# A later start for the splits of the last operands, a written order for the first tiles, and earlier requests for the gate's weights, in a one-layer decoder block

## The chip, the cores and the metric

The kernel runs on one core of one Trainium2 chip. The core has a matrix engine (TensorE), a vector engine (VectorE), an activation engine (ScalarE), a general one (GpSimd) and a queueing engine (SyncE) that here issues all transfers. The metric is the device time of one execution in microseconds (us), lower is better. Three timed runs of the kernel before gave 1779.38, 1779.62 and 1783.3 us; the median is 1779.62 us.

## The reference

One layer of a hybrid decoder on x of 1024 tokens by 1024 channels in float32:

```
u = rmsnorm(h, mix_pre_norm);  z = u @ w_in
o_attn = dilated_attention_branch(z_attn)      # 3 head groups, (window, dilation) (128,1), (512,4), (2048,16)
o_rwkv = rwkv7_time_mix(z_rwkv, ...)           # delta-rule state update, 8 heads of 64
gate_attn, gate_rwkv = split(sigmoid(z_gate), 2)
merged = gate_attn * (o_attn @ w_attn_up) + gate_rwkv * (o_rwkv @ w_rwkv_up)
h = h + rmsnorm(merged @ w_out, mix_post_norm)
f = rmsnorm(h, ffn_pre_norm)
f = square(relu(f @ w_ff_in)) @ w_ff_out       # 1024 -> 4096 -> 1024
h = h + rmsnorm(f, ffn_post_norm)
e = (p @ w_ple) * sigmoid(h @ w_ple_gate)      # p: 1024 x 256
h = h + rmsnorm(e, ple_post_norm)
```

## The kernel before

**Products in split parts.** A float32 operand is kept as a pair: hi, a copy rounded to the type fp32r, and lo, the rest. A product is three passes, hi·hi, lo·hi and hi·lo (lines 292, 294 and 296). A pair of a weight is made by ScalarE, which copies (hi), and GpSimd or VectorE, which subtracts (lo); wload (line 313) does this for one tile of 128 x 1024 (512 KB). Part of the second product of the MLP is done by a fast scheme with seven products for eight: product(n) (line 1546) takes pairs that prep (line 1536) makes of sums, in the tags Ep, En, a for the left side and kk, MP, px for the right side, taken in turn by n mod 3. The last two of the 32 row tiles of w_ff_out aren't in that scheme: ff2_last (line 1625) multiplies them in three passes.

**Stages, in time.** Head, 0 to about 35 us: the eight tiles of x are loaded, normalised and transposed (lines 354 to 437). Then the projections, the RWKV recurrence and the attention, to about 785 us. Then merge (line 1272), the product with w_out, ff1 (line 1563) with the products of the MLP's second half beside it, to about 1634 us. Then the end: ff2_last for eight token tiles, finish(i) (line 1710: norm, the residual h from scratch, transposition), gate_mm(i) (line 1730: the gate's product, 8 k-tiles in two halves of 512 columns) and e_mm(i) (line 1749: the last product, norm and output).

**The head.** stats(i) (line 387) squares tile i on ScalarE with its sum, and takes the root there and the reciprocal on VectorE. u_tile(i) (line 393) scales the tile by both on VectorE, has TensorE transpose it in two groups of four blocks (tp), and takes uh (ScalarE) and ul (VectorE) from each. z_quarter(n, q) (line 406) multiplies 256 tokens by the n-th of the first two weight tiles. keep_warm puts in small matmuls.

**Who sets the order.** TensorE's order over the whole kernel is planned by the program: bodies of matmuls (sch.add) and chains of other work (sch.spawn) are generators, the classes Engine and Loads (lines 79 to 133) add up modelled times for the other engines, and the next body or chain is picked by these. The order in which instructions stand in the source is that in which the plan reaches them. The other four engines keep that source order in two stretches alone: between the end of the head (lines 1227 and 1228) and the start of attention() (line 991), and from ff2_last(0, 0) (line 1635) to the end of the program. Elsewhere a scheduler orders them by its own rule from the source position and the state of their inputs and buffers.

**Parking.** Fourteen operands of the last stages are split long before they are used, by park() (line 968): two tiles of w_ple, two halves of p transposed, two tiles of w_ff_out and eight of w_ple_gate. Each is loaded raw into tag MP, split into a pair in tag BK2, and the pair is stored in a scratch tensor in device memory: pk[1] (in the profile pke), pk[2] (pkl) and pk[0] (pkg). The chain starts when ("vk", 1) is done: turn(1) (line 1015) of attention sets this when the second group of values is transposed into vkb. The event ("B", n) is set by values() at line 1113, when the last product po of values group n is done; merge also waits for ("B", 5) (line 1310).

**What is read back at the end.** last_split(1, ..) (line 1498) asks for the second row tile of w_ff_out: hi in a tag lw, and lo, "lwl", in tag MP. It is called behind product(103) (n == 7·NP − 9, NP = 16), in the last ff1 body. Inside ff2_last(0, 0) the program calls hl_load(0) (the residual tile, line 1706), opens the second stretch of source order, and calls last_weights (line 1658), which makes the tiles wpg for the gate's weights (first half of the columns in the tags TM0 and TM1, second half in mtile) and starts a chain that asks for their sixteen parts of 512 KB, first half first, paced by the modelled bus. When a half has landed it sets ("wpg", c); gate_mm waits for these.

Of the kernel before, what the change touches and what calls it, by code (L numbers as in the profile page):

```python
# [18 lines left out]
D = 1024  # L19
# [225 lines left out]
def layer(ctx: ExitStack, tc: tile.TileContext, x, pT, wz, wup, w_out, wff1, w_ff2, w_ple, w_pleg,  # L245
# [58 lines left out]
    def wait(cond):  # L304
        while not cond():
            yield 0.1
# [47 lines left out]
    with tc.tile_pool(name="xin", bufs=1) as xp:  # L354
        xts = [xp.tile([128, D], F32, name=f"xt{i}") for i in range(8)]

        def load_x(*tiles):
            for i in tiles:
                SY.dma_start(xts[i], x[i * 128:(i + 1) * 128, :])

        g1 = xp.tile([1, D], F32, name="g1")
        SY.dma_start(g1, gains[0:1, :])
        load_x(0, 1)
        cs = const.tile([128, N_CS0], F32, name="cs")
        SY.dma_start(cs, cst[:, 0:N_CS0])
        ident = cs[:, C_ID:C_ID + 128]
        eps = cs[:, C_EPS:C_EPS + 1]
        one = xp.tile([128, 128], F32, name="one")
        V.memset(one, 1.0)
        warm = xp.tile([1, 128], F32, name="warm")  # L370
        S.activation(warm, one[0:1], AF.Sqrt)
        def keep_warm(n):
            keep = zbank()[:, 0:128]
            for i in range(n):
                mm(keep, one, one, 0.107)

        keep_warm(4)
        g0 = xp.tile([128, D], F32, name="g0")
        for b, c in enumerate((slice(0, 512), slice(512, 1024))):
            ps = psum.tile([128, 512], F32, name="gb", tag=f"s{b + 2}")  # L380
            mm(ps, one[0:1], g1[:, c], 0.86)
            V.tensor_copy(g0[:, c], ps)
        keep_warm(7)
        tp = [0]
        ub = {}

        def stats(i):
            ss = small.tile([128, 1], F32, name="ss")
            us = xp.tile([128, D], F32, name="us", bufs=4)
            S.activation(us, xts[i], AF.Square, accum_out=ss)  # L390
            ub[i] = us, rstd_of(ss, "rs")

        def u_tile(i):
            h, ts = i // 4, slice((i % 4) * 128, (i % 4) * 128 + 128)
            us, r = ub[i]
            V.scalar_tensor_tensor(us, xts[i], r, g0, op0=OP.mult, op1=OP.mult)
            for b in range(2):
                ps = psum.tile([128, 4, 128], F32, name="tp", tag=("m0", "m1", "s1", "s2")[tp[0] % 4])
                tp[0] += 1
                for k in range(4):  # L400
                    tr(ps[:, k, :], us[:, (4 * b + k) * 128:(4 * b + k + 1) * 128], 0.11)
                o = (slice(None), slice(4 * b, 4 * b + 4), ts)
                S.activation(uT[0][h][o], ps, AF.Copy)
                V.tensor_tensor(uT[1][h][o], ps, uT[0][h][o], OP.subtract)

        def z_quarter(n, q):
            h, ts = q // 2, slice((q % 2) * 256, (q % 2) * 256 + 256)
            if q % 2 == 0:
                zl[h].append(psum.tile([128, 512], F32, name="z", tag="s3") if h and n else zbank())
            hi, lo = wl[n]  # L410
            now(mm3(zl[h][n][:, ts], [(hi[:, k * 128:k * 128 + 128], lo[:, k * 128:k * 128 + 128],
                                       uT[0][h][:, k, ts], uT[1][h][:, k, ts]) for k in range(KT)]))

        stats(0)
        stats(1)
        wl = [wload(wz[0])]
        load_x(2)
        u_tile(0)
        u_tile(1)
        keep_warm(2)  # L420
        stats(2)
        wl.append(wload(wz[1]))
        load_x(3, 4, 5, 6, 7)
        pr = const.tile([128, N_PRM], F32, name="pr")
        SY.dma_start(pr, prm)
        omu = const.tile([128, 14], F32, name="omu")
        V.tensor_scalar(omu, pr[:, 0:14], -1.0, 1.0, op0=OP.mult, op1=OP.add)
        oka = const.tile([128, NU], F32, name="oka")
        V.tensor_scalar(oka, pr[:, P_KA:P_KA + NU], -1.0, 1.0, op0=OP.mult, op1=OP.add)
        for q in range(4):  # L430
            z_quarter(0, q)
            for i in (2 * q + 2, 2 * q + 3):
                if i < 7:
                    stats(i + 1)
                if i < 8:
                    u_tile(i)
            z_quarter(1, q)

    rt = ctx.enter_context(tc.tile_pool(name="rt", bufs=1, reuse_waits="tile"))
    TAGN = {"BT": 2048, "TM0": 4096, "TM1": 4096, "AR0": 2048, "AR1": 2048, "BK": 2048, "BK2": 2048, "UV": 2048,  # L440
# [526 lines left out]

    def park():

        yield from wait(lambda: ("vk", 1) in done)  # L970
        rows = lambda w, k: w[k * 128:(k + 1) * 128, :]
        half = lambda h: pT[:, halves[h]].rearrange("(k p) c -> p k c", p=128)
        for dst, src in ([(pk[1][:, k], rows(w_ple, k)) for k in range(2)]
                         + [(pk[1][:, 2 + h], half(h)) for h in range(2)]
                         + [(pk[2][:, k], rows(w_ff2, FF // 128 - 2 + k)) for k in range(2)]
                         + [(pk[0][:, k], rows(w_pleg, k)) for k in range(KT)]):
            raw = rtile([128, 1024], "pkr", "MP")
            land = SY.dma_start(raw if len(src.shape) == 2 else k2(raw), src)
            yield max(land - sch.t, 0.0)
            t = rtile([128, 2, 1024], "pk", "BK2", F32R)  # L980
            S.activation(t[:, 0], raw, AF.Copy)
            yield 1.0
            V.tensor_tensor(t[:, 1], raw, t[:, 0], OP.subtract)
            yield sch.until(V.end)
            yield max(SY.dma_start(dst, t.bitcast(F32)) - sch.t, 0.0)
            yield 3.0
        done.add("park")

    def attention():
# [573 lines left out]
    def ff1(j):  # L1563
        def body(hi, lo):
# [4 lines left out]
            for h in range(0 if j > 2 else 1, 2):  # L1569
                ps = zbank()  # L1570
                g = ff1_half(ps, hi, lo, h)
                for k in range(2):
                    for _ in range(12):
                        yield next(g)
                    if k:
                        for _ in g:
                            pass
                        ff1_evac(ps, j, h)
                    for n in [x for _ in range(1 if j > 2 else 2) for x in (next(muls, None),) if x is not None]:
                        yield from product(n)  # L1580
                        if n in E_LOADS:
                            e_weights(E_LOADS.index(n))
                        if n == 7 * NP - 10:
                            last_split(0, (0, 1), (0,))
                        if n == 7 * NP - 9:
                            last_split(1, (0,), (1,))
# [38 lines left out]
    def ff2_last(i, c):  # L1625
        def body():
# [3 lines left out]
                                 last[k][1][:, halves[c]]) for k in range(2)])  # L1630
            V.tensor_tensor(acc(i, c), acc(i, c), ps, OP.add)
            if i + c == 0:
                hl_load(0)
                sch.exact = True
                last["turn"] = tc.manual_schedule(engines=OTHERS)
                last["turn"].__enter__()
# [11 lines left out]
    def e_weights(n):  # L1648
# [6 lines left out]
        else:  # L1655
            P[f"p{n - 2}"] = [k2(t[:, 0]), k2(t[:, 1])]

    def last_weights():
        pg = pieces(GA, "wpg", F32R)
        P["wpg"] = [[Split(pg[4 * p:4 * p + 4]), mtile("hl"[p], 0, [128, KT, 512], "wpg", F32R)]  # L1660
                    for p in range(2)]
        P["g3"] = rtile([128, D], "g3", "v")
        SY.dma_start(P["g3"], gains[3:4, :].to_broadcast([128, D]))

        def chain():
            land = 0.0
            for c in range(2):
                for k in range(0, KT, 2):
                    for p in range(2):
                        w = P["wpg"][p][c]  # L1670
                        yield max(SY.bus - 2.0 - sch.t, 0.0)
                        land = SY.dma_start((w.p[k // 2] if c == 0 else w[:, k:k + 2, :]).bitcast(F32),
                                            pk[0][:, k:k + 2, p, halves[c]])
                yield max(land - sch.t, 0.0)
                done.add(("wpg", c))
            e_weights(3)
        sch.spawn(chain(), 2)

# [51 lines left out]
    def gate_mm(i):  # L1730
        def body():
# [2 lines left out]
            hi, lo, t0 = hT[i]  # L1734
            wpg = P["wpg"]
            for c in range(2):
                while ("wpg", c) not in done:
                    yield 0.0
                ps = zbank()
                yield from mm3(ps, [(hi[:, k, :], lo[:, k, :], wpg[0][c][:, k, slice(0, 512)],  # L1740
# [3 lines left out]
                warm = small.tile([128, 1], F32, name="ss")  # L1744
                S.activation(warm, P["sg"][i % 4][:, D - 1:D], AF.Sqrt)
            done.add(("G", i))
        sch.add(body, None, lambda: ("wpg", 0) in done and i in hT and sch.t >= hT[i][2])

    def e_mm(i):
        def body():  # L1750
# [3 lines left out]
            for n, c in enumerate(cols):  # L1754
# [7 lines left out]
                S.activation(junk, sg[:, c], AF.Square, accum_out=sc[:, n:n + 1])  # L1762
                if n == 0 or i < 7:
                    (V if n else G).tensor_tensor(eg[:, c], sg[:, c], P["g4"][:, c], OP.mult)
            for c in cols[1:] if i == 7 else ():
                V.tensor_tensor(eg[:, c], sg[:, c], P["g4"][:, c], OP.mult)
            for n in range(1, len(cols)):
                V.tensor_tensor(sc[:, n:n + 1], sc[:, n - 1:n], sc[:, n:n + 1], OP.add)
            r = rstd_of(sc[:, n:n + 1], "rs")
            for c in cols:  # L1770
                V.scalar_tensor_tensor(sg[:, c], eg[:, c], r,
                                       acc(i, c.start // 512)[:, c.start % 512:(c.stop - 1) % 512 + 1], op0=OP.mult, op1=OP.add)
# [132 lines left out]
```

## Time and profile before

| what | us |
|---|---|
| median of three runs | 1779.62 |
| lowest and highest run | 1779.38, 1783.3 |
| the profiled execution | 1784.63 |
| its span (first to last instruction) | 1782.8 |
| mean granted TensorE clock | 0.993 of full |

All rows of the profile are of the one profiled execution, so their times add up to its span. A row of the timeline has the start, the duration, the engine, the line, the operation with output and inputs, the shapes, and in brackets the idle time of its engine just before and what ended it. "xN" is a count of instructions in the row. PE is TensorE, PEld its loading of weights, DVE VectorE, ACT ScalarE, POOL GpSimd, SPq the queue of SyncE. Line 113 is the helper through which all instructions of VectorE, ScalarE and GpSimd pass, and line 132 that of the transfers, so groups are told apart by the names of their tiles. A row of the waits says which instruction of TensorE waited for which engine's work, how long in total, how many times, and the longest.

### The profile page before, as it was taken

Reading aid. Unit: us, or ns where it says so; the run is one execution under the profiler, and the core shown is the slowest. Engines: PE = TensorE matmul, PEld = TensorE weight load, DVE = VectorE, ACT = ScalarE, POOL = GpSimd, SP = SyncE. Lnnn points to the kernel's source line nnn. Section 1 sums busy time; section 2 is a strip of 40 time slices with the busy share of each in tenths; the row PEclk is TensorE's granted clock in tenths of the full one; section 3 lists DMA queues with packets and bytes.
Section 4 is the critical chain, followed back from the end, with each engine's and each line's share of the span. In section 5 each row is a group of like instructions: output and inputs, shape, how many; then the busy total and the mean of one; then the engine's idle time right before and its main releaser. Section 6 shows DMA issues by size and latency. Waiting matters only on the chain. (4 is left out here: it accounts for less than half of the span.)

```text
span 1782.8 us, 25896 instructions
## 1 busy us (share of the span) xinstructions
PE 1751.7 (98%) x10192; PEld 1431.0 (80%) x10192; DVE 1069.6 (60%) x1880; ACT 733.1 (41%) x1301; POOL 735.0 (41%) x485
## 2 busy tenths in 40 slices
PE   9999989999999999999999999999999999999998
PEld 8787877878877777777888888888888888888786
DVE  6289776757546343342744655565565677888643
ACT  5833333332345444452533533333333333333353
POOL 1354131221222323322230276666666797893211
PEclk9999999999999999999999999999999999999999
DMA  4621121212375543232632321111211121114611
GB/s 162 210 95 36 49 77 43 90 42 91 111 246 191 183 166 95 84 133 104 208 132 97 110 80 51 48 55 41 76 55 48 48 72 48 48 36 165 219 48 47
DMA packets 59322, 175.49 MB, mean 98 GB/s; under 512 B 6849, under 2 KB 7233, under 8 KB 56898
## 3 DMA queue, kind: packets, MB, share of 16 engines
q1 hardware_dynamic: 59202, 173.85, 29.0%
q8 instruction: 80, 1.31, 0.3%
q14 instruction: 40, 0.33, 0.1%
HBM read 125.20 MB, written 41.94 MB: 94 GB/s over the span
## 5 line engine op out<-in xcount | busy, mean ns | idle before, releaser
L113 DVE TENSOR_TENSOR tot<-tot,bk 128x512 f32<-128x512 f32 x468 | 308.1, 684 | 190.6 <-PE bk L296 189.8
L113 POOL TENSOR_TENSOR wl<-wr,wh 128x1024 fp32r<-128x1024 f32 (+1 forms) x87 | 211.5, 2431 | 436.2 <-ACT wh L113 412.2
L292 PE MATMUL z<-uh,wh 128*128 128x512 f32 (+1 forms) x800 | 314.9, 394 | 5.2 <-ACT part L113 3.0
L296 PE MATMUL z<-uh,wl 128*128 128x512 f32 (+1 forms) x800 | 314.5, 393 | 2.7 <-POOL wl L113 2.7
L294 PE MATMUL z<-ul,wh 128*128 128x512 f32 (+1 forms) x800 | 315.7, 395 | 0.0
L294 PE MATMUL z<-f,wh 128*128 128x512 f32 x496 | 193.1, 389 | 0.2 <-DVE f L113 0.2
L292 PE MATMUL z<-f,wh 128*128 128x512 f32 x496 | 193.2, 389 | 0.1
L296 PE MATMUL z<-f,wl 128*128 128x512 f32 x496 | 193.0, 389 | 0.0
L113 ACT ACTIVATE duo<-sum 128x512 fp32r<-128x512 f32 x150 | 90.5, 626 | 224.9 <-PE bk L296 113.3
L292 PEld LDWEIGHTS z<-uh,wh 128*128 128x128 f32 x800 | 152.6, 191 | 36.9 <-ACT part L113 3.5
L296 PEld LDWEIGHTS z<-uh,wl 128*128 128x128 f32 x800 | 152.6, 191 | 34.5 <-POOL wl L113 4.0
L294 PEld LDWEIGHTS z<-ul,wh 128*128 128x128 f32 x800 | 152.8, 191 | 30.7 <-issue 3.8
L292 PE MATMUL bk<-duo 128*128 128x512 f32 x420 | 163.4, 389 | 0.0
L294 PE MATMUL bk<-duo 128*128 128x512 f32 x420 | 163.4, 389 | 0.0
L296 PE MATMUL bk<-duo 128*128 128x512 f32 x420 | 163.4, 389 | 0.0
L113 POOL TENSOR_TENSOR duo<-sum,duo 128x512 fp32r<-128x512 f32 x75 | 100.7, 1343 | 95.6 <-ACT duo L113 95.6
L113 ACT ACTIVATE wh<-wr 128x1024 fp32r<-128x1024 f32 (+1 forms) x87 | 90.3, 1038 | 103.7 <-PE z L294 74.6
L113 POOL TENSOR_TENSOR sum<-w2r 128x512 f32<-128x512 f32 x75 | 99.1, 1321 | 65.1 <-DMA w2r<-in_w_ff_dram 60.3
L294 PEld LDWEIGHTS z<-f,wh 128*128 128x128 f32 x496 | 93.1, 188 | 19.8 <-DVE f L113 0.5
L292 PEld LDWEIGHTS z<-f,wh 128*128 128x128 f32 x496 | 93.1, 188 | 19.6 <-ACT f L113 0.3
L296 PEld LDWEIGHTS z<-f,wl 128*128 128x128 f32 x496 | 93.1, 188 | 19.3
L113 POOL TENSOR_TENSOR sum<-hr 128x512 f32<-128x512 f32 x75 | 97.6, 1310 | 4.8 <-DVE duo L113 3.1
(310 smaller groups left out, 3198.1 us busy)
## 6 DMA issues: line engine op xcount, KB each, us to landing
wr<-in_wz_dram SPq DMA_DIRECT2D x48, 512.0 KB, 4.0
wr<-in_wff_dram SPq DMA_DIRECT2D x31, 512.0 KB, 3.6
w2r<-in_w_ff_dram SPq DMA_DIRECT2D x30, 512.0 KB, 3.7
xt<-in_x_dram SPq DMA_DIRECT2D x16, 512.0 KB, 4.2
gscr<-gst SPq DMA_DIRECT2D x32, 256.0 KB, 2.1
pkg<-pk SPq DMA_DIRECT2D x8, 1024.0 KB, 4.5
g<-gscr SPq DMA_DIRECT2D x16, 512.0 KB, 4.2
wpg<-pkg SPq DMA_DIRECT2D x16, 512.0 KB, 6.6
```

The source lines that it names most:

```text
L113: return f(*a, **kw)
L292: PE.matmul(ps, ah, bh, start=i == 0, stop=False)
L294: PE.matmul(ps, ah, bl, start=False, stop=False)
L296: PE.matmul(ps, al, bh, start=False, stop=i == n - 1)
```

## The change

The change has four parts.

1. Head: VectorE, ScalarE and GpSimd (not SyncE) keep their source order from the first load to the last z_quarter. The scaling leaves u_tile and becomes scale(i), called right behind stats(i). Tiles 0 and 1 are squared and scaled before the first wload; the square of tile 2 and the second wload come before u_tile(0); the loads of parameters and omu, oka come behind the z_quarters.
2. park() waits for ("B", 5), and its pauses behind the store are shorter.
3. hl_load(0) and the eight requests for the first half of the gate's weights (first_weights) stand in ff1's last body, behind the evacuation of half 0. last_weights keeps the second half, and gate_mm waits for that one only.
4. Last output tile: two of the multiplications with g4 on VectorE move, one between the two small sums, the other between the root and the reciprocal.

```diff
+        first_turn = tc.manual_schedule(engines=OTHERS - {mybir.EngineType.SP})
+        first_turn.__enter__()
         g1 = xp.tile([1, D], F32, name="g1")
...
+        def scale(i):
+            us, r = ub[i]
+            V.scalar_tensor_tensor(us, xts[i], r, g0, op0=OP.mult, op1=OP.mult)
+
         def u_tile(i):
             h, ts = i // 4, slice((i % 4) * 128, (i % 4) * 128 + 128)
-            us, r = ub[i]
-            V.scalar_tensor_tensor(us, xts[i], r, g0, op0=OP.mult, op1=OP.mult)
+            us = ub[i][0]
...
-        stats(0)
-        stats(1)
+        for i in range(2):
+            stats(i)
+            scale(i)
         wl = [wload(wz[0])]
         load_x(2)
-        u_tile(0)
-        u_tile(1)
-        keep_warm(2)
         stats(2)
         wl.append(wload(wz[1]))
         load_x(3, 4, 5, 6, 7)
+        u_tile(0)
+        u_tile(1)
+        scale(2)
+        keep_warm(2)
+        for q in range(4):
+            z_quarter(0, q)
+            for i in (2 * q + 2, 2 * q + 3):
+                if i < 7:
+                    stats(i + 1)
+                    scale(i + 1)
+                if i < 8:
+                    u_tile(i)
+            z_quarter(1, q)
+        first_turn.__exit__(None, None, None)
...
     def park():
 
-        yield from wait(lambda: ("vk", 1) in done)
+        yield from wait(lambda: ("B", 5) in done)
...
-            yield max(SY.dma_start(dst, t.bitcast(F32)) - sch.t, 0.0)
-            yield 3.0
+            SY.dma_start(dst, t.bitcast(F32))
+            yield 1.0
...
                         ff1_evac(ps, j, h)
+                        if (j, h) == (2 * NP - 1, 0):
+                            hl_load(0)
+                            first_weights()
...
             if i + c == 0:
-                hl_load(0)
                 sch.exact = True
...
+    def wpg_load(c, k, p):
+        w = P["wpg"][p][c]
+        return SY.dma_start((w.p[k // 2] if c == 0 else w[:, k:k + 2, :]).bitcast(F32),
+                            pk[0][:, k:k + 2, p, halves[c]])
+
+    def first_weights():
+        pg = pieces(GA, "wpg", F32R)
+        P["wpg"] = [[Split(pg[4 * p:4 * p + 4])] for p in range(2)]
+        for k in range(0, KT, 2):
+            for p in range(2):
+                wpg_load(0, k, p)
+
     def last_weights():
-        pg = pieces(GA, "wpg", F32R)
-        P["wpg"] = [[Split(pg[4 * p:4 * p + 4]), mtile("hl"[p], 0, [128, KT, 512], "wpg", F32R)]
-                    for p in range(2)]
+        for p in range(2):
+            P["wpg"][p].append(mtile("hl"[p], 0, [128, KT, 512], "wpg", F32R))
...
-            land = 0.0
-            for c in range(2):
-                for k in range(0, KT, 2):
-                    for p in range(2):
-                        w = P["wpg"][p][c]
-                        yield max(SY.bus - 2.0 - sch.t, 0.0)
-                        land = SY.dma_start((w.p[k // 2] if c == 0 else w[:, k:k + 2, :]).bitcast(F32),
-                                            pk[0][:, k:k + 2, p, halves[c]])
-                yield max(land - sch.t, 0.0)
-                done.add(("wpg", c))
+            for k in range(0, KT, 2):
+                for p in range(2):
+                    yield max(SY.bus - 2.0 - sch.t, 0.0)
+                    land = wpg_load(1, k, p)
+            yield max(land - sch.t, 0.0)
+            done.add("wpg")
             e_weights(3)
...
-                while ("wpg", c) not in done:
+                while c and "wpg" not in done:
                     yield 0.0
...
-        sch.add(body, None, lambda: ("wpg", 0) in done and i in hT and sch.t >= hT[i][2])
+        sch.add(body, None, lambda: i in hT and sch.t >= hT[i][2])
...
-            for c in cols[1:] if i == 7 else ():
-                V.tensor_tensor(eg[:, c], sg[:, c], P["g4"][:, c], OP.mult)
+            scale = lambda c: V.tensor_tensor(eg[:, c], sg[:, c], P["g4"][:, c], OP.mult)
             for n in range(1, len(cols)):
+                if i == 7 and n == 2:
+                    scale(cols[1])
                 V.tensor_tensor(sc[:, n:n + 1], sc[:, n - 1:n], sc[:, n:n + 1], OP.add)
-            r = rstd_of(sc[:, n:n + 1], "rs")
+            if i == 7:
+                r = small.tile([128, 1], F32, name="rs")
+                S.activation(r, sc[:, n:n + 1], AF.Sqrt, bias=eps, scale=1.0 / D)
+                scale(cols[2])
+                V.reciprocal(r, r)
+            else:
+                r = rstd_of(sc[:, n:n + 1], "rs")
```

More of the change, by code (lines that the diff above doesn't have):

```diff
@@ L429, in layer @@
         V.tensor_scalar(oka, pr[:, P_KA:P_KA + NU], -1.0, 1.0, op0=OP.mult, op1=OP.add)
[L430 to L437, printed above, removed]
     rt = ctx.enter_context(tc.tile_pool(name="rt", bufs=1, reuse_waits="tile"))
```

## The prediction

> **What bounds the kernel now.** I read the page's engine totals first, then TensorE's waits stage by stage, then the issue times of transfers, then windows of the three stretches that the change touches.
>
> ```profile
> span 1782.8 us, 25896 instructions
> PE 1751.7 (98%) x10192; PEld 1431.0 (80%) x10192; DVE 1069.6 (60%) x1880; ACT 733.1 (41%) x1301; POOL 735.0 (41%) x485
> ```
>
> TensorE is busy for 1751.7 of 1782.8 us. The change removes no matmul, so it can only close or open gaps on TensorE, and all gaps of the span together are 31 us. The waits of the three stretches (columns: who waited for whom, us in total, times, longest) are, for 0 to 45, 500 to 680 and 1600 to 1690 us:
>
> ```profile
> PE tp L283 <- DVE rs L113: 1.3, 1, 1.3
> PE tp L283 <- DVE us L113: 0.8, 1, 0.8
> ```
>
> ```profile
> PE yt L283 <- ACT rb L113: 2.0, 1, 2.0
> PE pt L283 <- ACT SB L113: 1.5, 2, 1.0
> PE z L292 <- ACT qk L113: 1.2, 1, 1.2
> PE sc L275 <- DVE qk L113: 1.1, 1, 1.1
> PE av L283 <- ACT v L113: 0.7, 1, 0.7
> ```
>
> ```profile
> PE z L294 <- DMA wpg<-pkg: 1.0, 1, 1.0
> PE bk L292 <- DVE tot L113: 0.9, 1, 0.9
> ```
>
> So the most that the change can win is 2.1 us in the head, part of 6.5 us around the splits, and 1.9 us before the gate. The question is what it wins of that and what it opens elsewhere.
>
> **The park edit (new wait for the last values of attention).** By its source the chain park() begins behind ("vk", 1). The trace says otherwise:
>
> ```profile
> 461.43 0.34 SPq L132 DMA_DIRECT2D pkr<-in_w_ple_dram  x1
> 480.60 1.06 ACT L113 ACTIVATE pk<-pkr 128x1024 fp32r<-128x1024 f32 x1 [7.87 <-PE wr L275]
> 565.49 0.58 ACT L113 ACTIVATE vkb<-av 128x512 f32<-128x512 f32 x1
> ```
>
> The copy that completes ("vk", 1) runs at 565.49, yet the first raw operand is asked for at 461.43 and the first split runs at 480.60, when TensorE lets go of the buffer. Outside the two stretches whose order is written out, an instruction of ScalarE, VectorE, GpSimd or SyncE thus starts when its buffer is free, not when the source reaches it. Moving the source start further back changes the instructions' rank, not their buffers (MP and BK2 have no user between). I therefore take the splits to stay near 480 to 667, and this edit to be worth 0. What it could win is seen here:
>
> ```profile
> 509.68 1.06 ACT L113 ACTIVATE pk<-pkr 128x1024 fp32r<-128x1024 f32 x1 [4.64 <-DMA pkr<-in_pT_dram]
> 512.82 0.66 PE L283 MATMUL yt<-cs,rb 128*128 128x128 f32 x4 [1.96 <-ACT rb L113]
> L113 ACT ACTIVATE pk<-pkr x14: 1039/1062/1079, 480.6 to 663.9; 128x1024 fp32r<-128x1024 f32 x14
> L113 DVE TENSOR_TENSOR pk<-pkr,pk x14: 1203/1225/3412, 485.0 to 667.0; 128x1024 fp32r<-128x1024 f32 x14
> ```
>
> ScalarE sits 4.64 us for a raw operand with rb queued behind it, and TensorE waits 1.96 us for rb. I count with it one wait for SB (1.0), the wait for qk on VectorE (1.1, beside the split of 3412 ns) and the other for SB (0.5): 4.6 of the 6.5 us. Bounds: -4.6 us if the splits really leave this stretch, 0 if they don't; the other end, if they land among the merges, is a rival below. The two changed yields of park (a shorter pause after the store) only alter the modelled plan: 0.
>
> **The gate's weights.** The eight first-half loads of wpg and hl_load(0) now stand in the source behind ff1's half (2·NP−1, 0), ahead of product(103), and so ahead of last_split(1, ..), which asks for lwl[1]. Before:
>
> ```profile
> 1616.75 3.29 SPq L132 DMA_DIRECT2D hl<-hscr  x3
> 1624.10 0.88 SPq L132 DMA_DIRECT2D wpg<-pkg  x2
> 1626.82 0.33 SPq L132 DMA_DIRECT2D lwl<-pkl  x1
> 1627.20 0.43 SPq L132 DMA_DIRECT2D wpg<-pkg  x1
> 1626.63 0.39 PE L292 MATMUL z<-f,wh 128*128 128x512 f32 x1
> 1635.69 0.39 PE L294 MATMUL bk<-lwl,lh 128*128 128x512 f32 x1
> L132 SPq DMA_DIRECT2D wpg<-pkg x16: 370/428/738, 1624.1 to 1673.8; - x16
> DMA to landing us min/median/max: 4.7/6.6/8.4
> ```
>
> lwl[1] goes to tag MP, which product(103) reads until 1626.63; it is asked for at 1626.82 and first needed near 1635.69. Its rank put it between wpg loads whose buffers were free already. Now all eight wpg loads outrank it. They issue from 1624.10 at about 0.4 us each, so the last is out by 1627.3 and lwl[1] is the ninth transfer. The rate of a full queue is in two windows (columns: window, length, busy time of PE, PEld, DVE, ACT, POOL, clock, DMA share, GB/s):
>
> ```profile
> 8.00:16.00 8.00, 7.18 (x34) 6.78 (x34) 7.16 (x8) 5.22 (x9) 2.36 (x1) 1.00 1.02 417
> 1647.00:1656.00 9.00, 9.00 (x45) 7.54 (x44) 7.20 (x14) 4.52 (x11) 3.25 (x2) 1.00 1.01 365
> ```
>
> 512 KB take 1.25 us at 417 GB/s and 1.44 at 365. First landing 1624.1 + 4.7 = 1628.8; eight transfers more: 1638.8 to 1640.3, against 1635.69. TensorE stalls for 3.1 to 4.6 us; I take **+4.0**, nearer to the second window, whose loads are the same ones. Below, the bound is 0 (lwl keeps its rank). Nothing hides the stall: on TensorE only the other ff2_last bodies follow, all of which read lwl[1]. hl_load(0), which moves too, adds nothing to the queue, since its loads were already out at 1616.75, ahead of their place in the source, like the splits.
>
> After such a pause the clock can fall:
>
> ```profile
> 149.00:153.00 4.00, 0.98 (x5) 0.50 (x3) 2.91 (x8) 3.96 (x6) 2.34 (x2) 0.97 0.01 4
> 153.00:156.00 3.00, 3.00 (x7) 2.35 (x8) 2.96 (x4) 1.92 (x3) 3.00 (x4) 0.50 0.00 0
> 500.00:530.00 30.00, 26.83 (x241) 21.85 (x241) 13.04 (x12) 12.87 (x18) 7.03 (x3) 1.00 0.75 264
> ```
>
> Behind 4 us in which TensorE was busy 0.98, it ran 3 us at clock 0.50; around the 1.96 us wait at 510 it stayed at 1.00. A 4 us stall is like the first, so I add half of 3 us: **+1.5**, bounds 0 and 3.4 (a spell of twice that length).
>
> [...]
>
> What the early loads remove: the wait for wpg (1.0) goes, since the second half's loads no longer queue behind the first half's. The wait of 0.9 for tot is one of a bank that VectorE's tile chain frees late; a TensorE that is 4 us later meets a VectorE that has caught up. **-1.9**, bounds -1.9 and 0.
>
> **The head.** The source order of VectorE, ScalarE and GpSimd now holds from the first load to the last z_quarter, and the scaling of u is moved ahead of wload's split.
>
> ```profile
> 7.88 1.28 DVE L113 SCALAR_TENSOR_TENSOR us<-xt,rs,g 128x1024 f32<-128x1024 f32 x1
> 9.27 3.33 DVE L113 SCALAR_TENSOR_TENSOR us<-xt,rs,g 128x1024 f32<-128x1024 f32 x1
> 9.17 2.36 POOL L113 TENSOR_TENSOR wl<-wr,wh 128x1024 fp32r<-128x1024 f32 x1 [8.71 <-ACT wh L113]
> 11.02 0.60 ACT L113 ACTIVATE uh<-tp 128x512 fp32r<-128x512 f32 x1 [1.93 <-PE tp L283]
> ```
>
> The second scaling took 3.33 us instead of 1.28, and for 2.36 us of it GpSimd's subtraction ran. Run clear of it, it would save up to 2.05, and the two waits (1.3 and 0.8) are what it feeds. Against that, ScalarE now has to do the third tile's square and the second weight's copy, both fed by loads, before the first uh at 11.02: these two cost up to 1 us each, and make uh about 1 us later. In the middle of the head, the scalings of tiles 4 and 6 now stand ahead of the uh/ul pairs that the next z_quarter needs; a scaling is 1.28 us, half of it covered, at two places: +1.2. So -2.1 (waits gone) +1.2 = **-0.9**, bounds -2.5 and +1.0. omu and oka move behind the head: nobody reads them there, 0.
>
> **The tail.** Two multiplications of the last tile fill VectorE's gaps between small steps:
>
> ```profile
> 1777.06 0.29 ACT L113 ACTIVATE rs<-sc,cs 128x1 f32<-128x1 f32 x1 [0.70 <-DVE sc L113]
> 1777.39 0.16 DVE L113 RECIPROCAL rs<-rs 128x1 f32<-128x1 f32 x1 [0.36 <-ACT rs L113]
> ```
>
> One of the two now stands where VectorE idles 0.36 us ahead of the reciprocal: **-0.2**, bounds -0.4 and 0.
>
> **The sum.** -0.9 + 0 + 4.0 + 1.5 - 1.9 - 0.2 = +2.5 us. The profiled execution took 1784.63 us (span 1782.8 and 1.83 around it), so it would take 1787.1. It lies 5.0 above the median of the runs, 1779.62, and the runs will be compared by medians: **1782.1**. Bounds of its own terms: from -2.5 + 0 + 3.1 + 0 - 1.9 - 0.4 = -1.7 to 1.0 + 4.6 + 3.4 - 0 = +9.0; not all ends meet, so I give it 1779 to 1786.
>
> **The rivals.** (a) *No halving behind the stall*: +1.0, so 1780.6. [...] Against: the row at 149.
> (b) *The burst does not get ahead of lwl*, because the transfers are interleaved as before or the buffers of the wpg come free later: -0.9 - 1.9 - 0.2 = -3.0, 1776.6. For it: lwl went out between wpg loads before. Against: it outranked them then.
> (c) *The splits do leave attention and the merges absorb them*: -4.6 more, 1777.5 with the stall, 1772.0 without it. Against: start at 480.60 with a source position at 565.
> (d) *Slower: the splits land in the merges and close their loop.* It holds if they start behind 785.
>
> ```profile
> 840.00:905.00 65.00, 65.00 (x289) 53.80 (x288) 45.68 (x63) 32.39 (x40) 14.99 (x8) 1.00 0.55 190
> 888.13 1.27 DVE L113 TENSOR_TENSOR g<-g,bk 128x512 f32<-128x512 f32 x2
> 889.11 0.39 PE L292 MATMUL bk<-orw,wh 128*128 128x512 f32 x1
> ```
>
> There TensorE has no gap, but the bank that it takes at 889.11 is freed by the first of the two g products, at 888.13 + 0.6 = 888.7: 0.4 us of slack. A split puts 1.225 us on VectorE and 1.06 on ScalarE in front of it, so from the first one that falls there each merge can lose 0.7 to 2 us; 14 splits spread over 5 merges at about 1.8 are +9. With attention's 4.6 won and the stall, 1779.62 + 2.5 - 4.6 + 9 = 1786.5.
> (e) *A longer stall or spell* (every term of the end at its upper bound): 1779.62 - 0.9 + 4.6 + 3.4 + 0 - 0.2 = 1786.5, and above that with the head at +1.0: 1788.4.
>
> **How the numbers follow.** Chances: forecast 0.32, (a) 0.15, (b) 0.24, (c) 0.14 (half with the stall), (d) 0.09, (e) 0.06. About 0.3%, 5.3 us, is what a measurement of this kernel can tell from no change: faster is below 1774.3, slower above 1785.0. Faster: (c) without stall 0.07, the low third of (b) 0.08, the low end of (c) 0.03: 0.18. Slower: the top quarter of the forecast 0.08, (d) 0.07, (e) 0.06: 0.21. The rest, 0.61, is within. Cases of both signs hold most of the chance; the range is 1772.5 to 1787.5, which leaves out half of the fastest case and the top of (d) and (e).
>
> **What would show it.** The issue rows of wpg and lwl: eight wpg from 1624 and lwl[1] behind them, and a TensorE wait for lwl of 3 to 5 us near 1635, show the stall; a clock of 0.50 in the window behind it shows the halving. First split of pk near 480 with the wait of yt for rb of about 2 us: park unmoved; a first split past 785 proves me wrong there, and then the waits between 840 and 905 decide between (c) and (d). In the head, a second us of 1.28 us and no wait of tp for rs. The prediction fails if lwl[1] is issued before the burst, or if the splits move.

## The result and the profile after

The kernel is slower. Six runs of each on one chip gave 1794.61 us (median, 1788.67 to 1797.33) for the changed kernel and 1779.95 us for the one before; the ratio is 1.0074 with a 95% interval of 1.0055 to 1.0094, that is 13 us, where +2.5 was forecast and the range ended at 1787.5. In the two profiled executions the span went from 1782.8 to 1792.7 us, 9.9 us more (the one of before lay 5 us above its median), and TensorE's busy time moved by 3.2:

```profile
span 1792.7 us, 25897 instructions
PE 1754.9 (98%) x10192; PEld 1433.9 (80%) x10192; DVE 1063.0 (59%) x1880; ACT 733.0 (41%) x1301; POOL 734.5 (41%) x485
```

Where the time went is read best from the start of the same TensorE row in both traces:

| TensorE row | before | after | later by |
|---|---|---|---|
| last tp of the head | 36.6 | 35.2 | -1.5 |
| last q of the recurrence | 499.7 | 498.2 | -1.5 |
| last av of attention | 756.1 | 761.1 | +5.0 |
| first bk<-duo of the MLP | 1030.9 | 1037.6 | +6.7 |
| first bk<-lw,lh of ff2_last | 1634.8 | 1641.4 | +6.7 |
| first z<-wpg,wh of the gate | 1670.4 | 1682.4 | +12.0 |
| last z<-wpg,wl | 1772.1 | 1782.8 | +10.7 |

So, between these two executions, the head wins 1.5, something in attention loses 6.5, the stretch up to the MLP another 1.7, with a new wait of tp for f of 1.5 in it, the opening of ff2_last 5.3, and the rest wins 1.3 again. The list of TensorE's waits of the changed kernel names them (waiting row, releaser, total, times, longest):

```profile
PE sc L275 <- DVE qk L113: 7.1, 2, 6.1
PE bk L294 <- DMA lwl<-pkl: 3.4, 1, 3.4
...
PE tp L283 <- DVE f L113: 1.5, 1, 1.5
PE z L294 <- DVE ul L113: 1.3, 3, 0.6
```

The wait for lwl is the one that was forecast. The wait of sc for qk was 1.1 us before and is now 7.1 in two, the longer one 6.1. It is no matter of the splits having moved; these stand where they stood (480.6 to 667.0 before):

```profile
L113 ACT ACTIVATE pk<-pkr x14: 1039/1061/1087, 479.1 to 659.3; 128x1024 fp32r<-128x1024 f32 x14
L113 DVE TENSOR_TENSOR pk<-pkr,pk x14: 1202/1225/3418, 483.5 to 667.4; 128x1024 fp32r<-128x1024 f32 x14
```

What moved is the order of others. The timeline of the changed kernel around the wait (start, duration, engine, operation, idle before and its end), on ScalarE, GpSimd, VectorE and TensorE:

```profile
652.96 1.23 DVE L113 TENSOR_TENSOR qk<-qk,rope 128x1024 f32<-128x1024 f32 x1 [7.95 <-DMA sw<-qk]
...
657.46 1.06 ACT L113 ACTIVATE wh<-wr 128x1024 fp32r<-128x1024 f32 x1 [4.15 <-PE z L294]
658.60 2.35 POOL L113 TENSOR_TENSOR wl<-wr,wh 128x1024 fp32r<-128x1024 f32 x1 [8.48 <-ACT wh L113]
660.90 2.35 POOL L113 TENSOR_TENSOR sw<-sw,rope 128x1024 f32<-128x1024 f32 x1
663.28 1.23 DVE L113 TENSOR_TENSOR qk<-qk,sw 128x1024 f32<-128x1024 f32 x1 [9.10 <-POOL sw L113]
664.56 1.66 PE L275 MATMUL sc<-qk 64*128 64x128 f32 x8 [6.05 <-DVE qk L113]
```

And the same instructions in the kernel before:

```profile
655.75 3.44 POOL L113 TENSOR_TENSOR sw<-sw,rope 128x1024 f32<-128x1024 f32 x1 [2.84 <-DMA sw<-qk]
659.22 1.22 DVE L113 TENSOR_TENSOR qk<-qk,sw 128x1024 f32<-128x1024 f32 x1 [2.29 <-POOL sw L113]
...
660.25 1.06 ACT L113 ACTIVATE wh<-wr 128x1024 fp32r<-128x1024 f32 x1 [4.16 <-PE z L294]
661.39 2.36 POOL L113 TENSOR_TENSOR wl<-wr,wh 128x1024 fp32r<-128x1024 f32 x1 [2.20 <-ACT wh L113]
664.83 0.93 PE L275 MATMUL sc<-qk 64*128 64x128 f32 x8
```

Before, GpSimd multiplies sw by the rotary table ahead of the weight's wl; after, wl stands first. Of the 485 instructions of GpSimd in both traces, these two alone stand in another order. wl needs wh, and wh needs a weight buffer that TensorE's z matmul (line 294) lets go of at 657. So GpSimd idles 8.48 us, for the last 5.6 of them with sw landed behind it (VectorE's wait for the same transfer ends at 652.96), and the scores wait for 1.06 + 2.35 + 2.35 + 1.23 us of work that can't begin before TensorE itself has come that far.

At the end, the requests are in the order that was forecast, eight loads of wpg ahead of lwl[1]:

```profile
1630.53 5.03 SPq L132 DMA_DIRECT2D wpg<-pkg  x8
1635.66 0.41 SPq L132 DMA_DIRECT2D lwl<-pkl  x1
```

```profile
1645.92 0.50 PE L294 MATMUL bk<-lwl,lh 128*128 128x512 f32 x1 [3.41 <-DMA lwl<-pkl]
```

### The profile page after: what moved, and what is told of

Read it like the earlier page. It is cut to its first block, busy times and chain, and to the rows that moved or that the text cites. A ratio compares the mean times of both kernels' runs of the same rounds, so it can differ in the third digit from the quotient of the medians.

```text
span 1792.7 us, 25897 instructions
## 1 busy us (share of the span) xinstructions
PE 1754.9 (98%) x10192; PEld 1433.9 (80%) x10192; DVE 1063.0 (59%) x1880; ACT 733.0 (41%) x1301; POOL 734.5 (41%) x485
```

## The experiments

Two theories were to be told apart from their rivals. P: park()'s edit, counted at 0, rewrites the plan of attention and with it GpSimd's order. B: the burst in front of lwl[1] costs the stall and a spell of half clock. All comparisons are with runs of the kernel before on the same chip.

| run | median, us | before, us | ratio (95%) |
|---|---|---|---|
| changed kernel | 1794.61 | 1779.95 | 1.0074 (1.0055 to 1.0094) |
| e1 park() alone | 1791.93 | 1781.59 | 1.0060 (1.0040 to 1.0079) |
| e2 all but park() | 1785.52 | 1781.59 | 1.0020 (1.0006 to 1.0034) |
| e3 lwl[1] ahead of the burst | 1787.53 | 1781.59 | 1.0038 (1.0024 to 1.0052) |
| e4 e2 and e3 together | 1778.01 | 1781.59 | 0.9977 (0.9964 to 0.9991) |
| e5 park()'s pauses alone | 1787.06 | 1781.67 | 1.0034 (1.0021 to 1.0047) |
| e6 one sw on VectorE | 1785.13 | 1781.67 | 1.0024 (1.0011 to 1.0038) |
| e7 splits really late | 1805.33 | 1781.67 | 1.0134 (1.0115 to 1.0153) |
| e8 head alone | 1780.66 | 1781.67 | 0.9999 (0.9986 to 1.0011) |
| e9 e3 and e6 together | 1781.31 | 1782.61 | 0.9993 (0.9982 to 1.0003) |
| e10 e4 again | 1779.58 | 1782.61 | 0.9977 (0.9962 to 0.9993) |

### e1: park() alone

```diff
 # the kernel before
-        yield from wait(lambda: ("vk", 1) in done)
+        yield from wait(lambda: ("B", 5) in done)
...
-            yield max(SY.dma_start(dst, t.bitcast(F32)) - sch.t, 0.0)
-            yield 3.0
+            SY.dma_start(dst, t.bitcast(F32))
+            yield 1.0
```

> The kernel before, with the edits to park() alone (condition and pauses). Theory P (the plan): with the splits gone from the modelled attention, TensorE's written order puts nine z matmuls less ahead of one group of scores, and GpSimd takes a weight's wl ahead of the sw of that group; the wait of sc for qk of about 6 us near 659, a spell of half clock behind it of about 2 us and the wait of tp for f near 1020 (1.5) appear, while the splits themselves stay between 480 and 667. From the changed kernel's lag against the kernel before, -1.5 us at 499 and +6.7 at 1031, that is +8 us: 1788. Rival (the prediction's step): the edit is worth 0, and the 6 us wait comes of the head, which shifts everything by 1.5 us: 1780.

The ratio of 1.0060 is +10.7 us. The wait is there with the same length, without any of the other edits:

```profile
PE sc L275 <- DVE qk L113: 7.1, 2, 6.0
```

That is theory P, and the rival (worth 0, the head does it) falls. In its trace the first bk<-duo is 7.2 us later than in the kernel before, and GpSimd's order is that of the changed kernel.

### e2: all but park()

> The changed kernel with park() as before. Theory P: no wait of sc for qk above 2 us; the head's -1.5, the stall for lwl with its half clock +5.3, the wait for wpg -1.0 and the tail -0.75 stay: +2 us against the kernel before, 1782. Rival: the 6 us wait is still there, about 1790.

+3.6 us, between the two numbers but with the mark of P: the longest wait of sc is the 1.1 us of the kernel before, and the wait for lwl (2.7) is there. The measured +3.6 is above the +2 worked out; the interval (1.0006 to 1.0034) takes +2 in.

### e3: lwl[1] ahead of the burst

```diff
 # the changed kernel
-                        if (j, h) == (2 * NP - 1, 0):
-                            hl_load(0)
-                            first_weights()
...
                             last_split(1, (0,), (1,))
+                            hl_load(0)
+                            first_weights()
```

> The changed kernel with hl_load(0) and the eight requests for the gate's weights set behind last_split(1, ..), so that lwl[1] is asked for ahead of the burst. Theory B (the burst): the wait of bk for lwl of 3.4 us goes, and the spell of half clock behind it (1.9) with it: 5.3 us less than the changed kernel, 1789; no wait for wpg comes in its place. Rival: the queue is full anyway and lwl or wpg is late by 1 to 3 us still: 1791 to 1793.

From 1.0074 to 1.0038, that is 6.4 us less, where 5.3 was expected. The waits of this kernel hold no line for lwl and none for wpg; SyncE asks for lwl[1] behind the first two wpg loads, as before, and seven more follow:

```profile
1628.90 0.89 SPq L132 DMA_DIRECT2D wpg<-pkg  x2
1631.85 0.33 SPq L132 DMA_DIRECT2D lwl<-pkl  x1
1632.23 8.14 SPq L132 DMA_DIRECT2D wpg<-pkg  x7
```

The weights of the gate come in time without going first. Theory B stands.

### e4 and e10: both mends, measured twice

The kernel of e2 with the edit of e3.

> The changed kernel with park() as before and lwl[1] ahead of the burst: what is left is the head, the earlier gate weights and the tail. Both theories together: -1.5 - 1.0 - 0.75 = -3.2 us against the kernel before, 1776.7. Rival: the parts don't add up, since the wait of tot for the bank grows, and it is within 1 us of the kernel before.

> The kernel of e4_both once more, on the same chip as e9: 0.9977 of the kernel before, 1777.5. If the gain in e4 was the luck of granted clock, it is 1.000.

Both gave 0.9977, about 4.1 us less than the kernel before (3.2 was worked out), and both intervals end below 1. Between 1600 and 1700 us its waits are one line, against two before:

```profile
PE bk L292 <- DVE tot L113: 0.9, 1, 0.9
```

This version beats both kernels: head, tail and early gate weights together pay once the burst is ranked behind lwl[1] and park() is left alone. How the gain is shared among the three isn't shown; the head alone gives none that can be measured (e8), and the wait for wpg and the tail account for 1.5 us.

### e5: park()'s pauses alone

```diff
 # the kernel before
-            yield max(SY.dma_start(dst, t.bitcast(F32)) - sch.t, 0.0)
-            yield 3.0
+            SY.dma_start(dst, t.bitcast(F32))
+            yield 1.0
```

> The kernel before, with park()'s shorter pauses behind the store alone; it still starts behind ("vk", 1). Theory P: any change of the modelled pauses rewrites TensorE's order in attention, not the start condition alone; here GpSimd again takes wl ahead of sw, but TensorE has eight z matmuls and one turn of values (some 2.7 us) more ahead of those scores than in the changed kernel, so the wait of sc for qk near 659 is 6.05 - 2.7 = 3.3 us, and the whole about +4 us against the kernel before: 1785. Rival: it is the start condition that does it, and the pauses are worth 0: no wait of sc above 1.2 us, 1781.6.

+6.1 us. The rival falls: pauses alone, with the start condition of before, bring the wait. But so does my number of 3.3: the wait is 6.04.

```profile
652.37 1.06 ACT L113 ACTIVATE wh<-wr 128x1024 fp32r<-128x1024 f32 x1 [4.15 <-PE z L294]
...
653.50 2.34 POOL L113 TENSOR_TENSOR wl<-wr,wh 128x1024 fp32r<-128x1024 f32 x1 [8.48 <-ACT wh L113]
655.81 2.33 POOL L113 TENSOR_TENSOR sw<-sw,rope 128x1024 f32<-128x1024 f32 x1
...
659.46 0.80 PE L275 MATMUL sc<-qk 64*128 64x128 f32 x4 [6.04 <-DVE qk L113]
```

I had miscounted the work ahead of the scores. In e5 as in the changed kernel, 5034 matmuls stand ahead of them, and they are the sixth behind the z matmul that frees the weight buffer; in the kernel before they are the 22nd, with eight av and eight z matmuls more in between. The chain wh, wl, sw, qk starts when that z matmul is done, so TensorE waits for something that it lets start itself, and the wait is the same 6.04 to 6.05 us in e1, e3, e5 and the changed kernel, which all have the scores at this place. The pauses thus changed two orders: GpSimd's, and TensorE's, where the scores come 16 matmuls sooner. How much of the length each makes can be estimated from the rows: from the start of that z matmul to the scores 664.83 - 659.77 = 5.06 us pass in the kernel before, and 664.56 - 656.99 = 7.57, of them 6.05 of wait, in the changed one. So the 16 matmuls are worth some 3.5 us, and GpSimd's exchange with TensorE's order of before would leave a wait of some 2.5. No run has that pairing. The start condition alone, with the long pauses, wasn't tried.

### e6: the one sw on VectorE

TensorE's order is that of the changed kernel in all 10192 matmuls; the plan still counts the multiplication on GpSimd.

```diff
 # the changed kernel
+            nsw[0] += 1
+            G.eng = nc.vector if nsw[0] == 8 else nc.gpsimd
             G.tensor_tensor(sw, sw, rope_t[g][:, 1], OP.mult)
+            G.eng = nc.gpsimd
```

> The changed kernel, with the one multiplication sw x rope that stood on GpSimd behind wl (the eighth of twelve) put on VectorE; TensorE's order is the same to the last matmul. Theory G (GpSimd's queue): sw landed before 653 and VectorE idles there, so qk is ready before TensorE comes to sc at 658: the wait of 6.05 us and its spell of half clock (about 2) go, and the kernel is 8 us faster than the changed one: 1786.5. Rival T (TensorE's order): the nine matmuls that went from ahead of the scores are the cause, and half of the wait or more (3 us) stays: 1790.

From 1.0074 to 1.0024, 8.9 us less. sw runs on VectorE at once, and qk is ready 1.9 us before TensorE comes to the scores at 653.15, which it does without a wait:

```profile
647.67 1.23 DVE L113 TENSOR_TENSOR sw<-sw,rope 128x1024 f32<-128x1024 f32 x1 [7.95 <-DMA sw<-qk]
...
650.06 1.23 DVE L113 TENSOR_TENSOR qk<-qk,sw 128x1024 f32<-128x1024 f32 x1
```

```profile
653.15 0.93 PE L275 MATMUL sc<-qk 64*128 64x128 f32 x8
```

Theory G is shown: with sw out of GpSimd's queue, the wait is gone. The rival (fewer matmuls ahead of the scores; 16 by the traces, not nine) falls as a cause of its own, since they are as few here. That it lengthens the wait once GpSimd's order is wrong is the estimate under e5.

### e7: the splits really late

```diff
 # the kernel of e3
-        yield from wait(lambda: ("B", 5) in done)
+        yield from wait(lambda: ("B", 5) in done and "sel" in done)
...
-            raw = rtile([128, 1024], "pkr", "MP")
+            raw = rtile([128, 1024], "pkr", "v")
...
         V.tensor_copy(sel.rearrange("p a b -> p (a b)"), sraw[0])
+        done.add("sel")
```

> The kernel of e3_lwl_first with the raw operands of park() in tag v instead of MP, which attention holds until its last step: the splits now can't start before about 795. Rival (c) of the prediction: attention loses the waits of yt, SB and qk beside the splits (about 4.6 us of the kernel before), no wait for sc of 6 us is there, and the merges absorb the splits: 1781.6 - 3.2 - 4.6 = 1774. Rival (d): the merges lose about 1.8 us each, +9 in all: 1783. Theory P says that the order of TensorE alone isn't the cost; so if GpSimd's order is that of before, no 6 us wait. A third place where it can fail: w3, the third weight of ff1, uses the tag BK2 behind the splits and can be late near 1010, by an unknown amount.

+23.9 us, worse than any case. The views of the waits for 500 to 680 and for 780 to 1030 us show both halves of the bargain:

```profile
PE z L292 <- ACT qk L113: 1.2, 1, 1.2
PE pt L283 <- ACT SB L113: 0.6, 1, 0.6
```

```profile
PE z L292 <- ACT w L113: 11.9, 1, 11.9
PE z L292 <- ACT mt L113: 3.1, 1, 3.1
PE bk L292 <- ACT wh L113: 2.7, 1, 2.7
PE z L296 <- DVE mt L113: 1.5, 1, 1.5
PE z L296 <- POOL w L113: 1.2, 1, 1.2
PE bk L296 <- POOL wl L113: 1.2, 1, 1.2
```

Attention's waits fall from 6.5 to 1.8 us, 4.7 less, against my 4.6. The merges and the first steps of w_out pay 3.1 + 2.7 + 1.5 + 1.2 = 8.5 for it, against 9 in rival (d). On top come 11.9 + 1.2 = 13.1 us for w3, which shares BK2 with the splits and gets it only behind the last of them:

```profile
1022.40 1.06 ACT L113 ACTIVATE w<-w 128x1024 fp32r<-128x1024 f32 x1 [5.36 <-DMA pkg<-pk]
```

And behind three of these waits the clock is halved: from 857 to 863, from 908 to 914 and up to 1031 TensorE is busy for 5.3, 3.5 and 5.8 us at a granted clock of 0.50 to 0.52, which costs some 7 us more.

Rival (c) falls. A split that leaves attention is paid for in the merges and again at w3.

### e8: the head alone

> The kernel before with the edit of the head alone; TensorE's order is unchanged from the first projection on. By the changed kernel's lag at 55 us (-1.5): 1.5 us less than the kernel before, 1780.1. The prediction's term was -0.9, with 0.5 to 0.6 us of new waits of z for ul at two places, which should show. Rival: the head's gain is lost again in the recurrence, where the waits hang on other engines: 0, 1781.6.

0.9999 (0.9986 to 1.0011): no difference that can be measured. TensorE's rows run 1.0 us ahead of those of the kernel before from 55 to 502 us, and at 541 us the lead is gone. Neither the lead nor its loss can be laid to the edit. The trace of e5, which hasn't the edit, ends its head 0.6 us ahead of this one (35.0 against 35.6). And the wait of yt for rb, 2.6 us here and 2.0 in the kernel before, is 2.4 in e4 and 0.3 in e10, which are one kernel. The interval allows up to 2.5 us of gain, so a gain of 1 to 1.5 isn't refuted either.

### e9: both mends, with park()'s edit left in

> The changed kernel with both mends and park()'s edit left in: the eighth sw x rope on VectorE and lwl[1] ahead of the burst. If the two mechanisms explain all of the loss, what stays is the head, the gate's weights and the tail (e4: 0.9977 of the kernel before) and the wait of tp for f near 1011 (1.5 us): 0.9985, about 1.4 us above e4_both's own time: 1779.0 against 1781.6. Rival: a third loss stands behind park()'s new plan that these don't mend, and it stays 4 us or more above e4_both: over 1782.

0.9993 (0.9982 to 1.0003): two mends that touch one multiplication and one place in the source take back the 13 us, as far as can be measured. It lies 2.9 us above e4 by the ratios, where 1.4 was expected, and the interval takes 0.9985 in. The rival (4 us or more above e4) isn't borne out, but the two intervals together leave room for it.

## Why the prediction was wrong

**The failed step** is the sentence on the park edit: "this edit to be worth 0", and beside it "the two changed yields of park ... only alter the modelled plan: 0". The first half of its reason held: the splits stayed at 479 to 667, as buffers rule and not the source. But the plan isn't only a record. TensorE's order and the source positions of all chains come out of the modelled times, and park()'s yields are part of these. With other pauses, the multiplication of one group's sw fell behind a weight's split in GpSimd's order, and TensorE came to that group's scores 16 matmuls sooner. The wait is 6.05 us, with 6.8 us of half clock at its end (from 663.25 us on in the changed kernel), and taking the multiplication out of GpSimd's queue gives 8.9 us back (e6), of the 10.7 of e1. The other 1.8 are less than the intervals can tell. The new wait of tp for f near 1020 isn't shown to be of park(): e10, with park() as before, has it, and e4, the same kernel, and e5, with the new pauses, haven't. This is the line of e10:

```profile
PE tp L283 <- DVE f L113: 1.4, 1, 1.4
```

I had asked what the moved instructions would collide with, and not what the planner would do with the time that it believed to be free.

**The burst** was right in mechanism and nearly in size: stall 4.0 forecast, 3.41 measured in the profile; half clock 1.5 forecast, 5.3 - 3.4 = 1.9 found (3.4 us at half the clock are 1.7 of it); together 5.5 against 5.3, and 6.4 by e3 (7.7 between e2 and e4). The bound of 3.4 set for the half clock is half of 6.8 us; the kernel before has such a spell, from 265.4 to 272.2 us. Only the details of the queue differ: eight requests took 5.03 us to issue instead of 3.2, and the loads came at 385 to 406 GB/s.

```profile
1639.00:1642.00 3.00, 3.00 (x15) 2.50 (x14) 0.86 (x2) 0.35 (x1) 0.00 (x0) 1.00 1.05 406
1642.00:1646.00 4.00, 0.59 (x4) 0.17 (x2) 0.69 (x1) 1.50 (x3) 0.00 (x0) 1.00 1.02 385
1646.00:1649.00 3.00, 3.00 (x8) 2.37 (x9) 0.69 (x1) 0.72 (x2) 0.00 (x0) 0.55 1.04 399
```

**The removed waits** were put at -1.9. The 1.0 for wpg went; the 0.9 of a bank for tot stayed in every kernel here, e4 too. That a later TensorE would meet a VectorE that has caught up was a guess without a row behind it.

**The head** was put at -0.9. Its last row is 1.5 us earlier in the profile, but no run shows this to be of the edit. The second scaling went from 3.33 to 1.28 us, as forecast:

```profile
9.28 1.28 DVE L113 SCALAR_TENSOR_TENSOR us<-xt,rs,g 128x1024 f32<-128x1024 f32 x1
```

But in e1 and e5, which have the head of the kernel before, it takes 1.28 and 1.29 us too, and the subtraction beside it is the long one. So it is in e5:

```profile
9.27 1.29 DVE L113 SCALAR_TENSOR_TENSOR us<-xt,rs,g 128x1024 f32<-128x1024 f32 x1
9.34 3.45 POOL L113 TENSOR_TENSOR wl<-wr,wh 128x1024 fp32r<-128x1024 f32 x1 [8.89 <-ACT wh L113]
```

In all twelve traces the one of the two that starts second is stretched (3.33 us of VectorE in the kernel before, 3.45 of GpSimd in e5). The subtraction started first in the profile of the kernel before alone, by 0.1 us, so the 3.33 us that the forecast took for a cost of the old order were those of one execution. The last tp of the head starts at 36.6 there, at 36.0 in e1 and 35.0 in e5 without the edit, and at 35.1 to 35.6 in the nine traces with it. What the edit does is to exchange waits: tp no longer waits for rs (1.3 to 1.5 us in the three traces without it), and z waits for ul for 1.3 us in three places (forecast 1.2 in two). As a time no gain of the head is measured (e8).

**The tail** was put at -0.2. In the changed kernel ScalarE's root waits 0.23 us for the sums instead of 0.70, and from the last sg to the last products pass 1787.84 - 1786.05 = 1.79 us, before 1777.66 - 1775.40 = 2.26: -0.47.

```profile
1787.24 0.29 ACT L113 ACTIVATE rs<-sc,cs 128x1 f32<-128x1 f32 x1 [0.23 <-DVE sc L113]
```

**The range** was too narrow by the same step: bounds of an edit on a plan have to hold what a shuffled order can cost, and the sizes of waits behind GpSimd (2.4 us for one subtraction) were in the page.

## What to carry to other kernels

Where a program writes one engine's order from modelled times, an edit of any modelled time is an edit of all orders: compare every engine's list of instructions before and after, and look first for an operation that has fallen behind one that waits for the bottleneck itself. In a queue, place a request by when its data are needed and not by when its buffer is free: one transfer that was due, behind eight of its size that were not, cost 5 to 8 us here, and the eight were needed some 35 us after it (1635.7 and 1670.4 in the kernel before). Before work is moved to a quieter stage, follow its buffers to their next user (w3 behind BK2: 13 us).

## What the runs showed of the hardware

In these traces a pause of TensorE could cost more than its length, and its length alone didn't decide whether it did. In e2 the stall for lwl was 2.73 us and the clock stayed at 1.00. Behind the 3.11 us of e6 and the 3.41 us of the changed kernel 3.4 us ran at half the clock, a loss of 1.7; at the end of the 6.04 us of e5 it was 6.8 us. But a wait of 2.37 us for rb in e4 was followed by half clock too (granted 0.56 from 507 to 510 us). And a pause of 3.0 us near 149 us is in all twelve traces: half clock follows it in eight of them (granted 0.56 from 152 to 155 us in the changed kernel), and in four, e2 among them (1.00 there), it doesn't.

```profile
148.00:152.00 4.00, 0.97 (x5) 0.49 (x4) 2.93 (x7) 3.96 (x6) 2.56 (x2) 1.00 0.02 4
152.00:155.00 3.00, 3.00 (x15) 2.47 (x14) 2.97 (x3) 1.71 (x3) 3.00 (x3) 1.00 0.00 0
1633.00:1636.00 3.00, 2.89 (x13) 2.40 (x14) 1.38 (x2) 0.75 (x3) 0.00 (x0) 1.00 1.05 394
```

```profile
504.00:507.00 3.00, 0.86 (x4) 0.38 (x2) 1.34 (x2) 1.66 (x3) 0.00 (x0) 1.00 0.53 216
507.00:510.00 3.00, 2.77 (x9) 2.39 (x10) 1.63 (x3) 1.72 (x3) 0.00 (x0) 0.56 0.95 309
```

```profile
1634.00:1637.00 3.00, 2.65 (x9) 2.12 (x10) 0.69 (x1) 0.72 (x2) 0.00 (x0) 0.80 1.02 389
1637.00:1640.00 3.00, 3.00 (x10) 2.34 (x10) 1.81 (x5) 1.55 (x4) 0.00 (x0) 0.63 0.98 378
```

```profile
659.00:662.00 3.00, 2.54 (x13) 1.90 (x14) 1.26 (x8) 0.00 (x0) 0.00 (x0) 0.50 0.03 5
662.00:665.00 3.00, 3.00 (x11) 2.51 (x10) 1.62 (x5) 2.56 (x9) 0.00 (x0) 0.50 0.21 87
```

(The first three rows are of e2, the next two of e4, then two of e6 and two of e5; the clock is the third number from the end.)

What else decides it isn't shown; no run here tests it.

The second thing not expected is how far single executions lie apart: e4 and e10, one kernel, had runs from 1770.65 to 1783.59 us. In the profiled executions the mean granted clock goes from 0.988 (e7, with its long pauses) to 0.996 (e2). Of the other kernels much of the difference arises between 150 and 530 us, in the recurrence with its many short pauses, though up to there the order of TensorE is the same in all of them: the matmul ahead of the wait for rb starts at 510.5 in the kernel before, at 509.0 in the changed kernel, but at 505.5 in e2 and 504.5 in e4, which have the same head. A part of under 2 us can't be weighed from one profile of this kernel.
